# Feed-forward part with ScalarE and VectorE in written order, gelu and product written later, weight sums at a pair's first split

## The chip, the cores and the metric

The kernel runs on one core of one Trainium2 chip. Its time is the device time of one launch in microseconds, taken as the median of several runs. One more execution was recorded by the hardware profiler; all rows of the trace come from that one.

## The reference

Two layers of a decoder, 512 tokens, width 1024, all in float32. Each layer has a part with four token mixers and then a gated feed-forward part; only the second is touched here. `D_FF` is 2816, so gate and value have 22 blocks of 128 channels each.

```python
hf = rms_norm(x, norm_ffn_pre[l])
u = causal_depthwise_conv(hf @ ffn_w_up[l], ffn_conv_w[l], ffn_conv_b[l])   # 3 taps
gate, val = jnp.split(u, 2, axis=-1)
f = (jax.nn.gelu(gate, approximate=True) * val) @ ffn_w_down[l]
x = x + rms_norm(f, norm_ffn_post[l])
```

## The kernel before

**Split numbers.** Every float32 matmul is made of three: operands are split into a rounded high part (ScalarE, a copy) and the rest (VectorE, a subtraction), and hi x hi, lo x hi and hi x lo are summed in PSUM. Weights arrive by SP's DMA queue in units of 128x1024 in three `raw` buffers and are split into four pairs of buffers `whi`, `wlo`. `w_get` takes the next unit, `w_ahead(n)` writes the splits up to n units ahead, `w_split` does it. Activations are split by `hilo` (L316); `hT_hi` and `hT_lo` hold the normed input, channels on the partitions.

**Pairs.** The up projection runs over 22 pairs i = 0..21, one block of gate (s = 0) and one of value (s = 1). Pairs 0 and 1 are made by `head`, which works while the norm before is still coming in. Of the others, 8 are full pairs: two projections `proj` of 24 matmuls of 512 columns. The 12 pairs in `SEVEN` (i from 4 to 20, those not divisible by 3) are made by `seven`: the 2x2 block product (two halves of the channels, two halves of the tokens) by seven half products instead of eight (`product`, 12 matmuls of 256 columns). For that, sums of weight blocks are formed by POOL in `w_seven` (units `fs`, n = 0..3), and sums of input blocks in `forms(h)`, h = 0, 1, as tiles ta..tf, split into t1..t4 (forms d1, d2, d4, d3). Three banks take the products, named sa, sb, se; ScalarE copies an intermediate state of `ba` three times (L1392, L1399, L1405) before the next product is accumulated into it, and VectorE adds (L1396, L1410, L1416). The last two products of a seven-pair, `four` and `three`, are not made at once: they are put into `rest`, and `more()` takes one from it between the products of the next pair.

**After a pair**, `ffn_pair` (L1311) scales both banks on ScalarE (L1316), adds two taps each on VectorE (L1319, 4 in all), applies gelu on ScalarE (L1321) and multiplies on VectorE (L1322). `split_act` splits finished products already, up to six. The down projection is the function `boundary`, which also makes the norm and starts the next layer.

**Order.** SP's queue is always in the written order. For the other engines a planner (the Tile scheduler, with its own estimates of time) reorders what is written, unless a stretch is put under `manual_schedule`: then the engine's queue is in the written order. In the feed-forward part before, that holds for TensorE alone, from after pair 1 to the tail of the down projection; ScalarE, VectorE and POOL are in the planner's order. There are helpers for writing things later: `later(us, fn)` puts a piece into `due`, and `pump(us)`, called after some microseconds' worth of matmuls, counts it down and writes it when its time has come; `bg` is a queue of pieces that `pump` writes when a rough count of VectorE's work (`dve(us)`, `behind()`) is below a bound.

Of the kernel before, what the change touches and what calls it, by code (L numbers as in the profile page):

```python
# [21 lines left out]
NP_ = DFF // 128  # L22
# [54 lines left out]
SLACK0 = 0.6  # L77
SLACK2 = 1.5
MAXB = 1.5

SEVEN = {i for i in range(4, NP_ - 1) if i % 3}

# [23 lines left out]
def build(tc, x, wts, prm, gains, cst, out, order=None):  # L106
# [5 lines left out]
    with ExitStack() as ctx:  # L112
# [14 lines left out]
        def slot(w=512, dt=F32, name="g"):  # L127
            return pg.tile([128, w], dt, tag="g", bufs=NG, name=nm(name))
# [41 lines left out]
        def halves(i, *srcs):  # L170

            hi = pw.tile([128, WMAX], F32R, tag="whi", bufs=NSPL, name=nm("whi"))
            lo = pw.tile([128, WMAX], F32R, tag="wlo", bufs=NSPL, name=nm("wlo"))
            c = 0
            for s, n in srcs:
                A.activation(hi[:, c:c + n], s, AF.Copy)  # L176
                V.tensor_tensor(lo[:, c:c + n], s, f(hi[:, c:c + n]), op=ALU.subtract)  # L177
                c += n
            parts[i] = (hi, lo)

        def w_seven(i):


            _, p, n = order[i][1]
            if n == 0:
                sums[p] = [i]
                halves(i, (raw[i], 1024))
            elif n == 1:
                r1, r2 = raw.pop(sums[p].pop()), raw[i]
                s1, s2, s4 = slot(name="s1"), slot(name="s2"), slot(name="s4")  # L190
                sums[p] += [s4, i]
                G.tensor_tensor(s1, r2[:, 0:512], r2[:, 512:1024], op=ALU.add)  # L192
                G.tensor_tensor(s2, s1, r1[:, 0:512], op=ALU.subtract)
                G.tensor_tensor(r2[:, 0:512], r1[:, 0:512], r2[:, 0:512], op=ALU.subtract)  # L194
                G.tensor_tensor(s4, r1[:, 512:1024], s2, op=ALU.subtract)  # L195
                halves(i, (s2, 512), (s1, 512))
            elif n == 2:
                halves(i, (raw.pop(sums[p].pop()), 1024))
            else:
                halves(i, (sums.pop(p)[0], 512))  # L200

        def w_split(q, roomy=False):

# [112 lines left out]
        def hilo(src, scale=1.0, name="hl"):  # L316
            dve(0.62)
            hi = slot(dt=F32R, name=name + "h")
            lo = slot(dt=F32R, name=name + "l")
            if scale == 1.0:  # L320
                A.activation(hi, src, AF.Copy)
                V.tensor_tensor(lo, src, f(hi), op=ALU.subtract)
            else:
                A.activation(hi, src, AF.Copy, scale=scale)
                V.scalar_tensor_tensor(lo, src, scale, f(hi), op0=ALU.mult, op1=ALU.subtract)
            return hi, lo
# [269 lines left out]
        for l in range(L):  # L596
# [714 lines left out]
            def ffn_pair(i, bs):  # L1311
                w = lambda k, s: pr[:, P_FW + k * 44 + s * NP_ + i:P_FW + k * 44 + s * NP_ + i + 1]
                us = [slot(name="fu") for _ in range(2)]
                for s in range(2):
                    j = P_FB + s * NP_ + i
                    A.activation(us[s], bs[s], AF.Identity, scale=w(2, s), bias=pr[:, j:j + 1])  # L1316
                for d in (1, 2):
                    for s in range(2):
                        V.scalar_tensor_tensor(us[s][:, d:], bs[s][:, :512 - d], w(2 - d, s), us[s][:, d:],  # L1319
                                               op0=ALU.mult, op1=ALU.add)  # L1320
                A.activation(us[0], us[0], AF.Gelu_apprx_tanh)  # L1321
                V.tensor_tensor(us[1], us[0], us[1], op=ALU.mult)  # L1322
                fa[i] = us[1]

            hb = head(l, [("fu", 0), ("fu", NP_), ("fu", 1), ("fu", NP_ + 1)], hooks)
            ffn_pair(0, hb[0:2])
            ffn_pair(1, hb[2:4])
            ffn_order.enter_context(tc.manual_schedule(engines={E_T}))
            hb = None


# [1 line left out]
            def v2(t):  # L1333
                return t.rearrange("p (k t) -> p k t", k=2)
# [3 lines left out]
            def forms(h):  # L1338
                def block(t, k, q):
                    return f(t[:, k * 4 + h * 2:k * 4 + h * 2 + 2, q * 256:q * 256 + 256])  # L1340
                hi, lo = (lambda k, q: block(hT_hi, k, q)), (lambda k, q: block(hT_lo, k, q))
                a, b = slot(name="ta"), slot(name="tb")
                V.tensor_tensor(v2(a), hi(0, 1), hi(0, 0), op=ALU.subtract)
                V.tensor_tensor(v2(b), lo(0, 1), lo(0, 0), op=ALU.subtract)
                V.tensor_tensor(a, a, b, op=ALU.add)
                form["d1"].append(hilo(a, name="t1"))
                c = slot(name="tc")
                V.tensor_tensor(v2(c), hi(1, 1), v2(a), op=ALU.subtract)
                V.tensor_tensor(v2(c), v2(c), lo(1, 1), op=ALU.add)
                form["d2"].append(hilo(c, name="t2"))  # L1350
                d = slot(name="td")
                V.tensor_tensor(v2(d), hi(1, 0), v2(c), op=ALU.subtract)
                V.tensor_tensor(v2(d), v2(d), lo(1, 0), op=ALU.add)
                form["d4"].append(hilo(d, name="t4"))
                e, g = slot(name="te"), slot(name="tf")
                G.tensor_tensor(v2(e), hi(1, 1), hi(0, 1), op=ALU.subtract)
                G.tensor_tensor(v2(g), lo(1, 1), lo(0, 1), op=ALU.subtract)
                G.tensor_tensor(e, e, g, op=ALU.add)
                form["d3"].append(hilo(e, name="t3"))

            def side(n, kt):
                if n in form:
# [4 lines left out]
            def product(b, w, c, n, first):  # L1367

                o = b[:, 0:256]
                kw = {} if first else {"skip_group_check": True}  # L1370
                for kt in range(4):
                    hi, lo = side(n, kt)
                    k = c + kt * 128
                    mm(o, wc(w[0], k), hi, first and kt == 0, False, **kw)
                    mm(o, wc(w[0], k), lo, False, False, **kw)
                    mm(o, wc(w[1], k), hi, False, kt == 3, **kw)

            rest = []

# [4 lines left out]
            def seven(i):  # L1384


                ba, bb, be = bank("sa"), bank("sb"), bank("se")
                sa, sb = slot(name="ca"), slot(name="cb")
                L_, R_ = slice(0, 256), slice(256, 512)
                w0 = w_get(l, ("fs", i, 0))  # L1390
                product(ba, w0, 0, (0, 0), True)
                A.activation(sa[:, L_], ba[:, L_], AF.Copy)  # L1392
                more()
                w_ahead(2)
                product(bb, w0, 512, (1, 0), True)
                V.tensor_tensor(bb[:, L_], bb[:, L_], sa[:, L_], op=ALU.add)  # L1396
                w1 = w_get(l, ("fs", i, 1))
                product(ba, w1, 0, "d2", False)
                A.activation(sa[:, R_], ba[:, L_], AF.Copy)  # L1399
                w_ahead()  # L1400
                more()
                product(be, w1, 512, "d1", True)
                w2 = w_get(l, ("fs", i, 2))
                product(ba, w2, 0, "d3", False)
                A.activation(sb[:, L_], ba[:, L_], AF.Copy)  # L1405
                w_ahead()

                def four():
                    product(ba, w2, 512, "d4", False)
                    V.tensor_tensor(ba[:, R_], be[:, L_], sb[:, L_], op=ALU.add)  # L1410

                def three():
                    w3 = w_get(l, ("fs", i, 3))
                    product(be, w3, 0, (1, 1), False)
                    w_ahead(2)
                    V.tensor_tensor(bb[:, R_], be[:, L_], sa[:, R_], op=ALU.add)  # L1416
                    ffn_pair(i, [bb, ba])
                rest.extend((four, three))

            forms(0)  # L1420
            for i in range(2, NP_):
                if i == 3:
                    forms(1)
                if i in SEVEN:
                    seven(i)
                    continue
                bs = []
                for s in range(2):
                    b = bank()
                    run(proj(b, l, ("fu", s * NP_ + i)))  # L1430
                    bs.append(b)
                    more()
                ffn_pair(i, bs)
                if i >= 4:
                    split_act(fa, min(6, 2 * (i // 3)))
            while rest:
                more()
            form.clear()
            lastl = l == L - 1
            if not lastl:  # L1440
# [131 lines left out]
```

## Time and profile before

| | |
|---|---|
| time, median of 3 runs (lowest, highest) | 1957.84 us (1956.21, 1959.49) |
| the profiled execution: time, span | 1954.89 us, 1953.1 us |
| its granted TensorE clock, mean | 0.99 |
| busy: TensorE, VectorE, ScalarE, POOL | 97%, 73%, 49%, 16% |
| feed-forward part, layer 0: from the first projection of pair 2 to the down projection | 620.0 to 859.2 us |
| the same, layer 1 | 1587.0 to 1821.9 us |

A row of a group of instructions has line, engine, operation, output and input tiles, shape and count, then busy microseconds and mean nanoseconds of one, then the idle time of the engine just ahead of them and what ended it. A row of the timeline or of the chain begins with the start and the length in microseconds. A row of the waits gives the sum, the count and the longest. In the table of windows the columns are stretch, length, busy time (and count) of TensorE, its weight loads, VectorE, ScalarE and POOL, the granted clock, the DMA share and GB/s. Matmuls are pipelined: their listed length is longer than the distance from one to the next, so rates are taken from long stretches.

### The profile page before, as it was taken

The numbers are of one execution on the slowest core, as the hardware profiler recorded it, in microseconds if no ns is written. First come the engines' busy times: TensorE is split into PE (matmuls) and PEld (weight loads), VectorE is DVE, ScalarE is ACT, GpSimd is POOL, SyncE is SP. The second block draws the span as 40 slices with busy tenths as digits, with TensorE's granted clock in tenths as the row PEclk, the third lists the DMA queues.
The fourth block names the chain that finished last, engine by engine and source line by source line (L and its number), as shares of the span: only waits on it lengthen the run. The fifth ranks groups of instructions, "written<-read, shape, count | busy, mean of one in ns | idle before, by whom it ended". The sixth has DMA issues, their size and how long they took to land.

```text
span 1953.1 us, 27602 instructions
## 1 busy us (share of the span) xinstructions
PE 1885.1 (97%) x10236; PEld 1628.1 (83%) x10236; DVE 1418.7 (73%) x2546; ACT 965.1 (49%) x1840; POOL 312.2 (16%) x377
## 2 busy tenths in 40 slices
PE   7999999999999879999999999999999997999997
PEld 7988888888889778888898888888888897888886
DVE  6888789798558777764468887897975587667622
ACT  5557576623334455543345666775233435545521
POOL 1403300000004333400023033000000052243000
PEclk9999999999999999999999999999999998999999
DMA  8523311232353223234554233112323512223332
GB/s 291 154 76 98 108 57 55 68 98 87 102 192 106 65 87 98 87 112 140 160 188 141 72 103 108 49 58 73 97 81 118 206 66 87 87 87 99 128 119 76
DMA packets 74695, 209.10 MB, mean 107 GB/s; under 512 B 11072, under 2 KB 11456, under 8 KB 74560
## 3 DMA queue, kind: packets, MB, share of 16 engines
q1 hardware_dynamic: 67392, 192.65, 30.4%
q0 software_dynamic: 7168, 14.69, 3.0%
q8 instruction: 80, 1.31, 0.3%
q14 instruction: 55, 0.45, 0.1%
HBM read 184.23 MB, written 8.39 MB: 99 GB/s over the span
## 4 chain that ended last, share of the span: by engine, by line
PE 80%; issue 7%; DVE 6%; POOL 3%; ACT 3%; DMA 1%; SPq 0%; DVEq 0%; POOLq 0%; ACTq 0%
PE ps L293 43%; PE tk L293 15%; PE sa L293 5%; PE o L293 3%; PE hd L293 3%; PE se L293 2%; PE vt L293 2%; PE sB L293 1%; PE sA L293 1%; DVE fu L1319 1%; PE tr L382 1%; DVE wlo L233 1%; POOL raw L194 1%; POOL s L195 1%; ACT fu L1316 1%
## 5 line engine op out<-in xcount | busy, mean ns | idle before, releaser
L232 ACT ACTIVATE whi<-raw 128x1024 fp32r<-128x1024 f32 (+2 forms) x270 | 254.8, 948 | 483.7 <-PE ps L293 270.6
L233 DVE TENSOR_TENSOR wlo<-raw,whi 128x1024 fp32r<-128x1024 f32 (+2 forms) x270 | 297.9, 1107 | 243.0 <-ACT whi L232 241.2
L293 PE MATMUL ps<-hT_hi,whi 128*128 128x512 f32 x1104 | 438.5, 397 | 0.8 <-DVE ob L1092 0.8
L293 PE MATMUL ps<-hT_hi,wlo 128*128 128x512 f32 x1104 | 435.4, 394 | 0.0
L293 PE MATMUL ps<-hT_lo,whi 128*128 128x512 f32 x1104 | 434.0, 393 | 0.0
L293 PEld LDWEIGHTS ps<-hT_hi,wlo 128*128 128x128 f32 x1104 | 207.8, 188 | 47.1
L293 PEld LDWEIGHTS ps<-hT_hi,whi 128*128 128x128 f32 x1104 | 208.1, 188 | 43.9 <-DVE ob L1092 1.7
L293 PEld LDWEIGHTS ps<-hT_lo,whi 128*128 128x128 f32 x1104 | 208.0, 188 | 42.9
L895 DVE SCALAR_TENSOR_TENSOR acc<-ct,prm,acc 128x511 f32<-128x511 f32 (+14 forms) x240 | 175.6, 732 | 3.4
L293 PE MATMUL tk<-whi,fh 128*128 128x512 f32 x336 | 131.0, 390 | 0.0
L293 PE MATMUL tk<-whi,fl 128*128 128x512 f32 x336 | 130.8, 389 | 0.0
L293 PE MATMUL tk<-wlo,fh 128*128 128x512 f32 x336 | 130.8, 389 | 0.0
L177 DVE TENSOR_TENSOR wlo<-raw,whi 128x1024 fp32r<-128x1024 f32 x48 | 72.8, 1520 | 71.0 <-ACT whi L176 71.0
L348 POOL TENSOR_TENSOR sm<-sm,mhalf 128x1 f32<-128x1 f32 x32 | 22.2, 694 | 557.5 <-DVE sm L347 557.5
L176 ACT ACTIVATE whi<-raw 128x1024 fp32r<-128x1024 f32 x48 | 50.6, 1060 | 87.0 <-issue 30.3
L1052 ACT ACTIVATE P<-P,sm 128x256 f32<-128x256 f32 (+3 forms) x128 | 70.6, 554 | 29.7 <-DVE sm L1050 28.0
L929 POOL TENSOR_TENSOR sm<-sm,mhalf 128x1 f32<-128x1 f32 x8 | 6.1, 762 | 479.7 <-DVE sm L927 472.6
L192 POOL TENSOR_TENSOR s<-raw 128x512 f32<-128x512 f32 x24 | 32.7, 1361 | 265.6 <-DMA raw<-wts 265.6
L293 PEld LDWEIGHTS tk<-whi,fl 128*128 128x128 f32 x336 | 63.1, 188 | 13.2
L293 PEld LDWEIGHTS tk<-wlo,fh 128*128 128x128 f32 x336 | 63.1, 188 | 12.9
L293 PEld LDWEIGHTS tk<-whi,fh 128*128 128x128 f32 x336 | 63.1, 188 | 12.9
L293 PE MATMUL sa<-t2h,whi 128*128 128x256 f32 x96 | 32.2, 336 | 42.1 <-ACT ca L1392 42.1
(352 smaller groups left out, 4612.0 us busy)
## 6 DMA issues: line engine op xcount, KB each, us to landing
raw<-wts SPq DMA_DIRECT2D x260, 512.0 KB, 3.6
raw<-wts SPq DMA_DIRECT2D x66, 256.0 KB, 2.6
br<-wts SPq DMA_DIRECT2D x40, 256.0 KB, 6.2
xr<-x SPq DMA_DIRECT2D x16, 256.0 KB, 5.0
gain<-gains SPq DMA_DIRECT2D x16, 256.0 KB, 5.5
Q<-hlh POOLq DMA_DIRECT2D x64, 64.0 KB, 2.5
Q<-hll POOLq DMA_DIRECT2D x64, 64.0 KB, 2.9
raw<-wts SPq DMA_DIRECT2D x8, 408.0 KB, 5.1
```

What stands on the lines that cost most here:

```text
L176: A.activation(hi[:, c:c + n], s, AF.Copy)
L177: V.tensor_tensor(lo[:, c:c + n], s, f(hi[:, c:c + n]), op=ALU.subtract)
L192: G.tensor_tensor(s1, r2[:, 0:512], r2[:, 512:1024], op=ALU.add)
L194: G.tensor_tensor(r2[:, 0:512], r1[:, 0:512], r2[:, 0:512], op=ALU.subtract)
L195: G.tensor_tensor(s4, r1[:, 512:1024], s2, op=ALU.subtract)
L232: A.activation(hi[:, c:c + n], s, AF.Copy)
L233: V.tensor_tensor(lo[:, c:c + n], s, f(hi[:, c:c + n]), op=ALU.subtract)
L293: T.matmul(o, lhsT=lhsT, rhs=rhs, start=start, stop=stop, **kw)
L348: G.tensor_tensor(v[:, 1:2], v[:, 0:1], mhalf[:, 0:1], op=ALU.pow)
L382: T.transpose(bs[t, h][:, k * 128:k * 128 + 128], y[h][:, k * 128:k * 128 + 128], ident)
L895: V.scalar_tensor_tensor(acc[i][:, k:], ct[i][:, :512 - k], w[:, 30 - k:31 - k], acc[i][:, k:], op0=ALU.mult, op1=ALU.add)
L1052: A.activation(P[i], P[i], AF.Exp, bias=mn[:, i:i + 1], scale=-1.0, accum_out=sm[:, i:i + 1])
```

## The change

- ScalarE and VectorE are put in the written order too, and this begins ahead of pair 0's and pair 1's `ffn_pair`; it ends where TensorE's ended before, in the tail of the down projection.
- In `ffn_pair` the taps are written bank by bank, and gelu and product are written later: after 4.2 and 5.7 us worth of matmuls. `product` now calls `pump`, so that this count goes on.
- `w_seven` writes a seven-pair's four weight sums with its first split (n = 0) instead of its second, with the last two exchanged.
- `forms` puts its VectorE operations and splits into `bg`; both halves are written before pair 2, and what is left is written ahead of the first seven-pair.
- `four` and `three` of a seven-pair that is followed by a full pair are now made in the middle and at the end of that pair's first projection (before: after the first and after the second). `split_act` is written between the two projections. In `seven` one `w_ahead()` becomes `w_ahead(2)`, and in `three` L1416 is written ahead of `w_ahead(2)`.

```diff
--- before.py
+++ after.py
@@ -77,6 +77,9 @@
 SLACK0 = 0.6
 SLACK2 = 1.5
 MAXB = 1.5
+
+T_G = 4.2
+T_M = 5.7
 
 SEVEN = {i for i in range(4, NP_ - 1) if i % 3}
 
@@ -183,21 +186,21 @@
 
             _, p, n = order[i][1]
             if n == 0:
-                sums[p] = [i]
                 halves(i, (raw[i], 1024))
-            elif n == 1:
-                r1, r2 = raw.pop(sums[p].pop()), raw[i]
+                assert i + 1 in raw
+                r1, r2 = raw.pop(i), raw[i + 1]
                 s1, s2, s4 = slot(name="s1"), slot(name="s2"), slot(name="s4")
-                sums[p] += [s4, i]
                 G.tensor_tensor(s1, r2[:, 0:512], r2[:, 512:1024], op=ALU.add)
                 G.tensor_tensor(s2, s1, r1[:, 0:512], op=ALU.subtract)
+                G.tensor_tensor(s4, r1[:, 512:1024], s2, op=ALU.subtract)
                 G.tensor_tensor(r2[:, 0:512], r1[:, 0:512], r2[:, 0:512], op=ALU.subtract)
-                G.tensor_tensor(s4, r1[:, 512:1024], s2, op=ALU.subtract)
-                halves(i, (s2, 512), (s1, 512))
+                sums[p] = [i + 1, s4, s1, s2]
+            elif n == 1:
+                halves(i, (sums[p].pop(), 512), (sums[p].pop(), 512))
             elif n == 2:
-                halves(i, (raw.pop(sums[p].pop()), 1024))
+                halves(i, (raw.pop(sums[p][0]), 1024))
             else:
-                halves(i, (sums.pop(p)[0], 512))
+                halves(i, (sums.pop(p)[1], 512))
 
         def w_split(q, roomy=False):
 
@@ -1314,18 +1317,27 @@
                 for s in range(2):
                     j = P_FB + s * NP_ + i
                     A.activation(us[s], bs[s], AF.Identity, scale=w(2, s), bias=pr[:, j:j + 1])
-                for d in (1, 2):
-                    for s in range(2):
+                dve(3.0)
+                for s in range(2):
+                    for d in (1, 2):
                         V.scalar_tensor_tensor(us[s][:, d:], bs[s][:, :512 - d], w(2 - d, s), us[s][:, d:],
                                                op0=ALU.mult, op1=ALU.add)
-                A.activation(us[0], us[0], AF.Gelu_apprx_tanh)
-                V.tensor_tensor(us[1], us[0], us[1], op=ALU.mult)
-                fa[i] = us[1]
+
+                def gelu():
+                    A.activation(us[0], us[0], AF.Gelu_apprx_tanh)
+
+                def times():
+                    dve(0.7)
+                    V.tensor_tensor(us[1], us[0], us[1], op=ALU.mult)
+                    fa[i] = us[1]
+                later(T_G, gelu)
+                later(T_M, times)
 
             hb = head(l, [("fu", 0), ("fu", NP_), ("fu", 1), ("fu", NP_ + 1)], hooks)
+            ffn_order.enter_context(tc.manual_schedule(engines={E_T, E_A, E_V}))
+            clk["dve"] = clk["pe"]
             ffn_pair(0, hb[0:2])
             ffn_pair(1, hb[2:4])
-            ffn_order.enter_context(tc.manual_schedule(engines={E_T}))
             hb = None
 
 
@@ -1339,24 +1351,28 @@
                 def block(t, k, q):
                     return f(t[:, k * 4 + h * 2:k * 4 + h * 2 + 2, q * 256:q * 256 + 256])
                 hi, lo = (lambda k, q: block(hT_hi, k, q)), (lambda k, q: block(hT_lo, k, q))
-                a, b = slot(name="ta"), slot(name="tb")
-                V.tensor_tensor(v2(a), hi(0, 1), hi(0, 0), op=ALU.subtract)
-                V.tensor_tensor(v2(b), lo(0, 1), lo(0, 0), op=ALU.subtract)
-                V.tensor_tensor(a, a, b, op=ALU.add)
-                form["d1"].append(hilo(a, name="t1"))
-                c = slot(name="tc")
-                V.tensor_tensor(v2(c), hi(1, 1), v2(a), op=ALU.subtract)
-                V.tensor_tensor(v2(c), v2(c), lo(1, 1), op=ALU.add)
-                form["d2"].append(hilo(c, name="t2"))
-                d = slot(name="td")
-                V.tensor_tensor(v2(d), hi(1, 0), v2(c), op=ALU.subtract)
-                V.tensor_tensor(v2(d), v2(d), lo(1, 0), op=ALU.add)
-                form["d4"].append(hilo(d, name="t4"))
-                e, g = slot(name="te"), slot(name="tf")
-                G.tensor_tensor(v2(e), hi(1, 1), hi(0, 1), op=ALU.subtract)
-                G.tensor_tensor(v2(g), lo(1, 1), lo(0, 1), op=ALU.subtract)
-                G.tensor_tensor(e, e, g, op=ALU.add)
-                form["d3"].append(hilo(e, name="t3"))
+                a, b, c, d, e, g = (slot(name="t" + n) for n in "abcdef")
+                sub, add = ALU.subtract, ALU.add
+
+                def op(o, x, y, how):
+                    def go():
+                        dve(0.62)
+                        V.tensor_tensor(o, x, y, op=how)
+                    bg.append(go)
+                op(v2(a), hi(0, 1), hi(0, 0), sub)
+                op(v2(b), lo(0, 1), lo(0, 0), sub)
+                op(a, a, b, add)
+                op(v2(c), hi(1, 1), v2(a), sub)
+                op(v2(c), v2(c), lo(1, 1), add)
+                bg.append(lambda: form["d1"].append(hilo(a, name="t1")))
+                op(v2(d), hi(1, 0), v2(c), sub)
+                op(v2(d), v2(d), lo(1, 0), add)
+                bg.append(lambda: form["d2"].append(hilo(c, name="t2")))
+                G.tensor_tensor(v2(e), hi(1, 1), hi(0, 1), op=sub)
+                G.tensor_tensor(v2(g), lo(1, 1), lo(0, 1), op=sub)
+                G.tensor_tensor(e, e, g, op=add)
+                bg.append(lambda: form["d4"].append(hilo(d, name="t4")))
+                bg.append(lambda: form["d3"].append(hilo(e, name="t3")))
 
             def side(n, kt):
                 if n in form:
@@ -1374,6 +1390,7 @@
                     mm(o, wc(w[0], k), hi, first and kt == 0, False, **kw)
                     mm(o, wc(w[0], k), lo, False, False, **kw)
                     mm(o, wc(w[1], k), hi, False, kt == 3, **kw)
+                pump(1.42)
 
             rest = []
 
@@ -1397,7 +1414,7 @@
                 w1 = w_get(l, ("fs", i, 1))
                 product(ba, w1, 0, "d2", False)
                 A.activation(sa[:, R_], ba[:, L_], AF.Copy)
-                w_ahead()
+                w_ahead(2)
                 more()
                 product(be, w1, 512, "d1", True)
                 w2 = w_get(l, ("fs", i, 2))
@@ -1412,29 +1429,31 @@
                 def three():
                     w3 = w_get(l, ("fs", i, 3))
                     product(be, w3, 0, (1, 1), False)
+                    V.tensor_tensor(bb[:, R_], be[:, L_], sa[:, R_], op=ALU.add)
                     w_ahead(2)
-                    V.tensor_tensor(bb[:, R_], be[:, L_], sa[:, R_], op=ALU.add)
                     ffn_pair(i, [bb, ba])
                 rest.extend((four, three))
 
             forms(0)
+            forms(1)
             for i in range(2, NP_):
-                if i == 3:
-                    forms(1)
                 if i in SEVEN:
+                    while bg:
+                        bg.popleft()()
                     seven(i)
                     continue
                 bs = []
                 for s in range(2):
                     b = bank()
-                    run(proj(b, l, ("fu", s * NP_ + i)))
+                    for k, _ in enumerate(proj(b, l, ("fu", s * NP_ + i))):
+                        if k % 2 == 1 and s == 0:
+                            more()
                     bs.append(b)
-                    more()
+                    if s == 0 and i >= 4:
+                        split_act(fa, min(6, 2 * (i // 3)))
                 ffn_pair(i, bs)
-                if i >= 4:
-                    split_act(fa, min(6, 2 * (i // 3)))
-            while rest:
-                more()
+            flush()
+            assert not rest and not bg
             form.clear()
             lastl = l == L - 1
             if not lastl:
```

## The prediction

> **What bounds the kernel now.** I read the page first, for the engines:
>
> ```profile
> span 1953.1 us, 27602 instructions
> PE 1885.1 (97%) x10236; PEld 1628.1 (83%) x10236; DVE 1418.7 (73%) x2546; ACT 965.1 (49%) x1840; POOL 312.2 (16%) x377
> ```
>
> TensorE sets the time, so only its pauses and its slow stretches can be won. Then the waits, for the whole run and for each layer's feed-forward window (columns: total us, times, longest):
>
> ```profile
> PE sa L293 <- ACT ca L1392: 42.1, 12, 6.2
> ...
> PE sa L293 <- ACT ca L1392: 22.2, 6, 6.2
> ...
> PE sa L293 <- ACT ca L1392: 19.9, 6, 6.2
> ```
>
> All twelve pauses have one form: in the first of every two neighbouring seven-product pairs, product "d2" may not overwrite bank `ba` before ScalarE has copied its left half away (L1392). The chain shows one of them, and where the feed-forward part ends; the timeline shows where TensorE began it in each layer:
>
> ```profile
> 651.19 2.93 PE sa L293 x12
> 654.12 1.94 PE se L293 x12
> ...
> 784.84 4.32 issue
> 789.16 1.07 ACT whi L176
> 790.79 1.30 issue
> 793.89 1.45 ACT fu L1316 x2
> 795.66 1.70 PE sa L293 x12
> ...
> 798.80 4.30 PE sa L293 x36
> ...
> 810.26 5.60 PE ps L293 x24
> ...
> 859.20 111.56 PE tk L293 x492
> ```
>
> ```profile
> 620.03 0.40 PE L293 MATMUL ps<-hT_hi,whi 128*128 128x512 f32 x1
> 1587.04 0.40 PE L293 MATMUL ps<-hT_hi,whi 128*128 128x512 f32 x1
> 1821.92 1.16 PE tk L293 x5
> ```
>
> The unhindered rate is 4.30 us for 36 narrow and 5.60 for 24 wide matmuls. From pair 2 on a layer has 8 full pairs (16 x 5.60 = 89.6) and 12 seven-pairs (1008 narrow matmuls, 28 x 4.30 = 120.4): 210.0 us. It took 859.20 - 620.03 = 239.2 and 1821.92 - 1587.04 = 234.9. So 29.2 + 24.9 = 54.1 us are lost: 42.1 in pauses, 12.0 at a lower clock behind them. The windows show that clock:
>
> ```profile
> 651.00:656.00 5.00, 4.81 (x25) 4.81 (x26) 5.00 (x8) 4.00 (x8) 0.00 (x0) 0.59 0.12 15
> 793.00:800.00 7.00, 4.89 (x41) 4.68 (x40) 7.00 (x11) 5.18 (x10) 2.54 (x2) 1.00 0.48 150
> 827.00:834.00 7.00, 5.09 (x30) 4.95 (x29) 7.00 (x12) 4.33 (x9) 1.92 (x1) 0.76 0.38 140
> ```
>
> After the 6.2 us pause the clock was 0.59 and 24 narrow matmuls took 2.93 + 1.94 instead of 2.87: 2.0 us more. After a 2.1 us pause (793) it stayed at 1.00, after one of about 2 us (827) it fell to 0.76. The Trainium skill, "TensorE: Matmul & The Clock Gate", Part 1, gives an idle window of about 3.4 us before the clock halves; by that the short pause at 827 would have cost nothing further, and the row says that it did, so the row decides.
>
> **Why the copy is late.** In ScalarE's timeline, before L1392:
>
> ```profile
> 790.69 1.06 ACT L176 ACTIVATE whi<-raw 128x1024 fp32r<-128x1024 f32 x1 [0.47 <-PE se L293]
> 792.55 0.78 ACT L1316 ACTIVATE fu<-sb,prm 128x512 f32<-128x512 f32 x1 [0.80 <-DVE sb L1416]
> 793.23 0.77 ACT L1316 ACTIVATE fu<-sa,prm 128x512 f32<-128x512 f32 x1
> 793.89 1.45 ACT L1316 ACTIVATE fu<-ps,prm 128x512 f32<-128x512 f32 x2
> 795.21 0.39 ACT L1392 ACTIVATE ca<-sa 128x256 f32<-128x256 f32 x1
> ```
>
> ScalarE is 49% busy; it is not short of time. It stood behind weight splits that wait for a `whi` buffer still in use, then behind four scalings of two pairs at once: `three` of the old seven-pair and the full pair both end just before the new one starts.
>
> **The change, part by part.** Call one period F (full pair), C, D (seven-pairs), D' the D before. At the unhindered rate TensorE runs, from 0: F's first half 0 to 2.8, four(D') to 4.2, rest of that projection to 7.0, three(D') to 8.5, F's second projection to 14.1, then C's five products (last ends at 21.2), D(0,0) to 22.6, four(C), D(1,0), D d2 to 26.9, three(C) to 28.4, d1, d3 to 31.2. The written order of both queues follows from the new code. Prices, from the groups in 662 to 860 and (last row) the page's DMA issues:
>
> ```profile
> L177 DVE TENSOR_TENSOR wlo<-raw,whi 128x1024 fp32r<-128x1024 f32 x21 | 34.3, 1632 | 35.6 <-ACT whi L176 35.6
> L177 DVE TENSOR_TENSOR wlo<-s,whi 128x512 fp32r<-128x512 f32 x31 | 20.5, 677 | 0.0
> L233 DVE TENSOR_TENSOR wlo<-raw,whi 128x1024 fp32r<-128x1024 f32 x15 | 18.3, 1221 | 10.6 <-ACT whi L232 10.6
> L1319 DVE SCALAR_TENSOR_TENSOR fu<-sa,prm,fu 128x511 f32<-128x511 f32 (+1 forms) x22 | 16.2, 737 | 0.0
> L1322 DVE TENSOR_TENSOR fu<-fu,fu 128x512 f32<-128x512 f32 x16 | 13.8, 865 | 1.0 <-ACT fu L1321 0.5
> L1416 DVE TENSOR_TENSOR sb<-se,ca 128x256 f32<-128x256 f32 x12 | 5.1, 426 | 3.4 <-PE se L293 3.4
> L176 ACT ACTIVATE whi<-raw 128x1024 fp32r<-128x1024 f32 x20 | 21.2, 1061 | 42.7 <-issue 21.6 <-PE ps L293 13.8 <-PE sa L293 5.0
> raw<-wts SPq DMA_DIRECT2D x260, 512.0 KB, 3.6
> ```
>
> *Load.* A period gives VectorE 6 full splits (6 x 1.22), 6 half ones (6 x 0.68), 12 tap products (12 x 0.74), 3 gated products (at least 3 x 0.68, the uncontended length of a 512-wide operation) and 6 small sums (6 x 0.43): 24.9 of 31.2 us. Nothing is added, so order decides. 80% in strict order leaves about 6 us of slack.
>
> *L1392 of C.* Ahead of it on ScalarE now stand C1's and C2's splits, gelu(D') and F's two scalings. The splits' buffers are free by 8.5, so nothing there waits for F any more. VectorE reaches F's taps at about 14.8; F's second scaling follows the bank at 14.1 and ends at 14.9; L1392 follows product (0,0) at 15.5 and ends at 16.0. TensorE wants it at 16.9: about 1 us of slack, no pause. This takes away the steady pauses.
>
> *L1399 of C.* gelu(F) is now written ahead of it and waits for F's first two taps (16.1). L1399 follows d2 at 18.4, ends at 18.8, needed at 19.8: 1 us; F's taps could be 2.9 us later before it slips.
>
> *D0's split* is written behind L1399: ScalarE 18.8 to 19.8, VectorE to 21.1; D(0,0) needs the low part with its third matmul at 21.5. It is the tightest place: 0.4 us if VectorE is free and uncontended.
>
> *D2 and the next F split* (behind L1399 and three of D): done at 29.6 and 31.1, needed at 30.0 and 31.7: 0.4 and 0.6 us.
>
> *Banks.* L1410 must read `be` before three writes it. That distance shrinks in F from a whole second projection to half of one: ready at about 6, needed at 7.0.
>
> *Sums with the first split.* The four POOL operations come one split earlier; with the reordering `s4` is ready before the product that overwrites `raw`. SP's queue order stays; the first raw buffer is still read by the fourth operation, so D1's load starts at about 10, lands 3.6 later, and POOL works for D from 14 to 20. Its halves are wanted at 21.6. Cost nothing; if POOL slips by over a microsecond it shows as ScalarE waiting for L193.
>
> *Splits of gated products* (split_act): four in pair 6, two in pair 9, now inside the period, 4 x 0.68 on VectorE. They push D0 of seven-pair 7 past its need by about 1 us, once a layer.
>
> I take 0.5 us for each of the other five periods (between 0, where every slack holds, and 2.1, the pause that the row at 793 had at the same place), so 3.5 a layer.
>
> *The start.* Both `forms` now come before L1392 of pair 4. The chain before:
>
> ```profile
> 646.62 0.70 DVE td L1353
> ...
> 647.89 0.61 ACT t3h L321
> 648.50 1.04 ACT whi L176 x2
> 649.54 1.33 ACT fu L1316 x2
> 650.87 0.28 ACT ca L1392
> ```
>
> VectorE had been working without a break for it. In written order it must also have done, ahead of td(1), two half splits, one full split and pair 3's four taps: 1.2 + 1.2 + 2.7 = 5.1 (shown as later in the trace now); it is spared two waits of 0.7 for ScalarE, since `d` is written ahead of the t2 split. ScalarE in turn has its 2.4 us of splits and scalings behind it. So L1392 ends at 651.15 + 5.1 - 1.4 - 2.4 = 652.5, and the pause grows from 6.2 to about 7.6, plus 2.0 of clock: 9.6 a layer. Bounds: 6.2 (nothing gets later) and 11.3 (no relief).
>
> *The down projection* is in order too until its tail. Nothing there is late:
>
> ```profile
> 860.00:972.00 112.00, 112.00 (x500) 92.83 (x499) 52.83 (x70) 41.88 (x67) 2.09 (x3) 1.00 0.44 142
> ```
>
> VectorE at 47%, ScalarE at 37%, splits three units ahead: 0. If that cover were gone, a split late by x would cost x.
>
> **The sum.** Left per layer: 9.6 + 3.5 = 13.1. Won: 54.1 - 2 x 13.1 = 27.9. The profiled execution was 1954.89 (span 1953.1 and 1.8 around it), 0.15% under the median; 1957.8 - 27.9 = 1930 on the median's scale.
>
> **A rule that speaks against it.** VectorE operations beside POOL ones are longer here: the 1632 against the 1221 above, and 865 against 0.68. Over a layer that is 21 x 0.41 + 16 x 0.18 = 11.5 us, 1.9 a period. In the new order up to four such operations a period (two gated products, C0's and D0's low parts) fall into POOL's stretches, at 0.7 each 2.8, so 0.9 more, and at D0 it falls where there is no slack. The Trainium skill, "SBUF — State Buffer", Who interferes with whom, says that a VectorE instruction with two SBUF inputs and a GpSimd one that reads SBUF block each other fully; the 1632 agrees. If each period pays that 0.9 in full on top, 12 x 0.9 = 11 us go back: 1941.
>
> **The rivals.**
> 1. *Clean order* (0.15): no residue, first pause as before: 54.1 - 2 x 8.2 = 37.7 won, 1920; were the start to vanish as well, 1904. For it: VectorE has 6 us of slack a period. Against: three slacks of 0.4 to 0.6.
> 2. *Half the stalls stay* (0.20): port blocking at D0, or L1392 still late behind F's scalings. With 1.5 to 2.1 us in each period: 1941 to 1953. Here belongs also that the change does not cure what it aims at: F's scalings still stand ahead of L1392.
> 3. *Slower* (0.10): strict order makes gelu(F) hold L1399. VectorE would be late at F's taps; beyond 2.9 us each microsecond goes straight into TensorE's wait before d3. It decides from 27.9 / 12 = 2.3 us a period beyond that, so taps 5.2 late; at 3 us a period with 0.3 of clock it would be 1930 + 12 x 3.3 = 1970. For it: the four taps, two splits and a gated product come in one burst from 12 to 19. Against: 80% load.
>
> The forecast itself has 0.50 (own range 1918 to 1942), and 0.05 is no change: a run of rival 2 or 3 that ends within 0.2%, 3.9 us, about what a measurement of this kernel tells apart. Faster: 0.50 + 0.15 + 0.20 = 0.85. The range, 1908 to 1952, leaves out the best of rival 1 and the slow cases.
>
> **What would show it.** The wait "sa on L1392" falls from 42.1 to some 15 to 18 us, nearly all in two entries of 7 to 9 us; a small new wait of D(0,0) for L177; POOL's L192 early in each period; clock 1.00 in every stretch but the one behind pair 4. Wrong if ScalarE waits long for L1319 with L1399 behind it, if new entries of TensorE on L177 exceed 1 us a period, or if the first pause is beyond 11 us.

## The result, and the profile after

The changed kernel takes 1942.04 us (1939.32 to 1942.91) against 1957.03 in the same runs: ratio 0.992, interval 0.9903 to 0.9937. That is 15 us; 28 were forecast. From the page of the changed kernel:

```profile
PE 1880.2 (97%) x10236; PEld 1622.7 (84%) x10236; DVE 1437.0 (74%) x2546; ACT 955.6 (49%) x1840; POOL 313.6 (16%) x377
```

Its lines are renumbered: L1392, L1399, L1405, L1416, L1316, L1319, L1322 are now L1409, L1416, L1422, L1432, L1319, L1323, L1331. TensorE's waits, for each layer's feed-forward part:

```profile
PE sa L296 <- ACT ca L1409: 11.0, 1, 11.0
PE sa L296 <- ACT ca L1416: 3.5, 2, 3.2
PE sa L296 <- DVE wlo L180: 2.8, 4, 1.3
...
PE sa L296 <- ACT ca L1409: 9.5, 1, 9.5
PE sa L296 <- DVE wlo L180: 3.6, 5, 1.3
PE sa L296 <- ACT ca L1416: 3.5, 2, 3.2
```

Of the twelve pauses on the first copy, ten are gone. The two at pair 4 have grown from 6.2 to 11.0 and 9.5, and there are new ones on the second copy and on a low part. Where the parts begin (timeline) and end (chain):

```profile
620.82 0.40 PE L296 MATMUL ps<-hT_hi,whi 128*128 128x512 f32 x1
850.48 111.55 PE tk L296 x492
1577.38 0.40 PE L296 MATMUL ps<-hT_hi,whi 128*128 128x512 f32 x1
1808.46 91.60 PE tk L296 x404
```

The two layers take 229.7 and 231.1 us instead of 239.2 and 234.9, so 13.3 us less together, which is nearly the whole difference of the spans (13.5). Above twice the unhindered 210.0 there remain 40.7 us: 33.9 of pauses, and 6.8 that are put down to a lower clock. This sum of two lengths is used below for every kernel ("the part").

One steady period shows how strict order works. ScalarE's timeline:

```profile
781.98 0.78 ACT L1319 ACTIVATE fu<-sb,prm 128x512 f32<-128x512 f32 x1 [3.74 <-DVE sb L1432]
...
783.32 1.14 ACT L179 ACTIVATE whi<-s 128x512 fp32r<-128x512 f32 x2
```

and VectorE's:

```profile
781.51 0.43 DVE L1432 TENSOR_TENSOR sb<-se,ca 128x256 f32<-128x256 f32 x1
782.79 1.53 DVE L1323 SCALAR_TENSOR_TENSOR fu<-sb,prm,fu 128x511 f32<-128x511 f32 x2 [0.85 <-ACT fu L1319]
...
788.02 2.97 DVE L1323 SCALAR_TENSOR_TENSOR fu<-ps,prm,fu 128x511 f32<-128x511 f32 x4
...
792.70 1.98 DVE L180 TENSOR_TENSOR wlo<-raw,whi 128x1024 fp32r<-128x1024 f32 x1
```

ScalarE stands still for 3.74 us, up to 781.98, for three's sum. The next pair's two half splits stand behind it, though POOL has both of their inputs ready at 780.30 (L194, from 778.67 for 1.63 us). From 782.79 on VectorE has twelve microseconds of work without a gap, and D0's low part comes last (792.70 to 794.68): TensorE waits 0.48 us for it.

### The profile page after: what moved, and what is told of

It reads as the page before. It is cut to its first block, busy times and chain, and to the rows that moved or that the text cites. A ratio compares the mean times of both kernels' runs of the same rounds, so it can differ in the third digit from the quotient of the medians.

```text
span 1939.6 us, 27581 instructions
## 1 busy us (share of the span) xinstructions
PE 1880.2 (97%) x10236; PEld 1622.7 (84%) x10236; DVE 1437.0 (74%) x2546; ACT 955.6 (49%) x1840; POOL 313.6 (16%) x377
## 4 chain that ended last, share of the span: by engine, by line
PE 86%; DVE 9%; issue 2%; ACT 1%; DMA 1%; POOL 0%; SPq 0%; DVEq 0%; POOLq 0%; ACTq 0%
PE ps L296 45%; PE tk L296 16%; PE sa L296 5%; PE hd L296 5%; PE o L296 3%; PE se L296 3%; DVE wlo L180 3%; DVE fu L1323 2%; PE vt L296 2%; PE sB L296 1%; PE sA L296 1%; PE sb L296 1%; PE tr L385 1%; DVE fu L1331 1%; PE tB L1076 1%
## 5 line engine op out<-in xcount | busy, mean ns | idle before, releaser
L236 DVE TENSOR_TENSOR wlo<-raw,whi 128x1024 fp32r<-128x1024 f32 (+2 forms) x270 | 297.3, 1105 | 229.3 <-ACT whi L235 227.5
L1055 ACT ACTIVATE P<-P,sm 128x256 f32<-128x256 f32 (+3 forms) x128 | 70.6, 554 | 29.7 <-DVE sm L1053 28.0
L193 POOL TENSOR_TENSOR s<-raw 128x512 f32<-128x512 f32 x24 | 39.3, 1637 | 260.1 <-DMA raw<-wts 254.2
L580 POOL DMA_DIRECT2D Q<-hlh x64 | 31.6, 497 | 198.9 <-ACT hlh L324 189.8
L296 PE MATMUL hd<-hT_hi,bh 128*128 128x256 f32 x256 | 63.4, 285 | 0.0
```

The lines of the kernel that those rows point to most:

```text
L296: T.matmul(o, lhsT=lhsT, rhs=rhs, start=start, stop=stop, **kw)
L580: G.dma_start(f(dst[row:row + 32, :]), f(src[srow:srow + 32, :]))
L1055: A.activation(P[i], P[i], AF.Exp, bias=mn[:, i:i + 1], scale=-1.0, accum_out=sm[:, i:i + 1])
```

## The experiments

Ratios are to the kernel before, in the same runs. They answer four questions: order or move, POOL, the small slacks, the start.

**Order or move.** *order_only*, the kernel before plus

```diff
+            ffn_order.enter_context(tc.manual_schedule(engines={E_T, E_A, E_V}))
             ffn_pair(0, hb[0:2])
             ffn_pair(1, hb[2:4])
-            ffn_order.enter_context(tc.manual_schedule(engines={E_T}))
```

> The kernel before, with nothing changed but that ScalarE and VectorE are in the written order from pair 0 on. Theory O+M (order helps only with the pieces written where they fit): gelu stands right behind its own four taps and holds ScalarE for 3 us in each pair, L1392 gets later, pauses of 4 to 6 us in all twelve places, 1965 to 1990. Rival O alone (order is the whole gain): 1938 to 1946.

Measured 2014.09 us, ratio 1.0295 (1.0275 to 1.0314). On the old code, order alone costs 58 us: the waits on L1392 rise from 42.1 to 87.7. gelu stands right behind its taps, and the copy behind both (ScalarE's timeline, pair 7):

```profile
696.44 0.63 ACT L1321 ACTIVATE fu<-fu 128x512 f32<-128x512 f32 x1 [2.46 <-DVE fu L1319]
...
699.06 0.36 ACT L1392 ACTIVATE ca<-sa 128x256 f32<-128x256 f32 x1
```

*planner*, the changed kernel with

```diff
-            ffn_order.enter_context(tc.manual_schedule(engines={E_T, E_A, E_V}))
+            ffn_order.enter_context(tc.manual_schedule(engines={E_T}))
```

> The changed kernel, with ScalarE and VectorE given back to the planner in the feed-forward part; everything else of the change is kept (four and three moved, gelu and product later, sums first). Theory O (the strict order is what removes the steady pauses): the planner again puts scalings or splits ahead of the first copy, 4 to 6 pauses of 2 us a layer come back, 1948 to 1956 us. Rival M (the move of four and three is what counts, the order is not needed): 1934 to 1944, steady pauses on the copies below 8 us in sum.

Measured 1929.56 us, ratio 0.986 (0.9841 to 0.988): 12.5 us faster than with the order, and below the range of either theory. Its waits:

```profile
PE sa L296 <- ACT ca L1409: 13.6, 3, 11.3
...
PE sa L296 <- ACT ca L1409: 11.7, 2, 10.9
```

Hardly anything is left but the first pause. VectorE in the same period:

```profile
775.15 1.90 DVE L180 TENSOR_TENSOR wlo<-s,whi 128x512 fp32r<-128x512 f32 x2 [0.41 <-ACT whi L179]
776.98 0.42 DVE L1432 TENSOR_TENSOR sb<-se,ca 128x256 f32<-128x256 f32 x1
...
784.05 2.32 DVE L180 TENSOR_TENSOR wlo<-raw,whi 128x1024 fp32r<-128x1024 f32 x1
```

The pair's first product on TensorE, here and then in the changed kernel:

```profile
781.38 0.28 PE L296 MATMUL sa<-hT_hi,whi 128*128 128x256 f32 x1
```

```profile
786.82 0.28 PE L296 MATMUL sa<-hT_hi,whi 128*128 128x256 f32 x1
```

The next pair's two half splits stand ahead of three's sum here, and D0's low part is done at 786.37, 8.3 us earlier than with the order. Of this, 5.4 us are TensorE's own lead at this place (its pair begins at 781.38 and not 786.82); measured from the pair's beginning, the low part comes 2.9 us sooner, and TensorE does not wait for it. Theory O has fallen.

*move_only*, the kernel before plus

```diff
-                    run(proj(b, l, ("fu", s * NP_ + i)))
+                    for k, _ in enumerate(proj(b, l, ("fu", s * NP_ + i))):
+                        if k % 2 == 1 and s == 0:
+                            more()
                     bs.append(b)
-                    more()
```

> The kernel before with one edit: four and three are made in the middle and at the end of the full pair's first projection. Planner's order, gelu, product, sums and forms as before. Theory M (the move alone takes the steady pauses away; the rest of the change costs): first pause 6.2 a layer as before, the other ten pauses (29.7 us and some 8 of clock) nearly gone, 1918 to 1932. Rival (gelu and product later, or the sums first, are needed as well): 1940 to 1957.

Measured 1924.63 us, ratio 0.983 (0.9815 to 0.9844). This small edit gives 32 us, twice the whole change. Waits:

```profile
PE sa L293 <- ACT ca L1392: 10.2, 3, 6.3
...
PE sa L293 <- ACT ca L1392: 11.1, 3, 6.2
```

The pause at pair 4 is as before, the later ones are 3.9 and 4.9 us a layer, 8.8 of the 29.7 us before. So the move alone takes most of the steady pauses away; what else is in the change costs about 17 us in sum.

**POOL.** *sums_second*, the changed kernel with `w_seven` as it was before.

> The changed kernel with the weight sums written at the second split again. POOL's queue starts them when the raw units land, whichever split writes them, so theory: within 4 us of the changed kernel (1938 to 1946), POOL's first sum still waits for the DMA. Rival (the earlier writing is what makes the order possible): ScalarE waits for POOL at the halves, 1950 to 1960.

Measured 1942.49 us, ratio 0.9923 (0.9904 to 0.9942): no difference. The earlier sums buy nothing under strict order. Nor does the exchange of the last two: POOL is not in the written order, and in the changed kernel's trace L196 still runs ahead of L195.

*no_sums*, the changed kernel without POOL's four weight sums; three memsets take their place, so it does not compute the layer's result:

```diff
-                G.tensor_tensor(s1, r2[:, 0:512], r2[:, 512:1024], op=ALU.add)
...
+                for s_ in (s1, s2, s4):
+                    G.memset(s_, 0.01)
```

> The changed kernel with POOL's four sums of a seven-pair left out: three memsets take their place, so POOL writes and reads nothing, and the weights of the second to fourth unit are not the sums. Theory P (the remainder, 34 us of pauses, is in good part VectorE held up by POOL's reads): the 512-wide splits next to POOL fall from 1.7 to 0.7 us, first pause of a layer 11 to 6 or 7 us, steady ones 6 to 2 a layer, 1924 to 1933 us. Rival (strict order alone makes the pauses, POOL costs nothing): 1938 to 1943.

Measured 1923.37 us, ratio 0.9828 (0.9811 to 0.9845): 18.7 us less. VectorE's groups in layer 0's part, changed kernel and then this one:

```profile
L180 DVE TENSOR_TENSOR wlo<-raw,whi 128x1024 fp32r<-128x1024 f32 x24 | 36.2, 1508 | 17.8 <-ACT whi L179 17.8
L180 DVE TENSOR_TENSOR wlo<-s,whi 128x512 fp32r<-128x512 f32 x36 | 27.2, 794 | 1.0 <-ACT whi L179 1.0
L1331 DVE TENSOR_TENSOR fu<-fu,fu 128x512 f32<-128x512 f32 x22 | 24.0, 1097 | 0.0
```

```profile
L180 DVE TENSOR_TENSOR wlo<-raw,whi 128x1024 fp32r<-128x1024 f32 x24 | 29.3, 1221 | 20.8 <-ACT whi L179 20.8
L180 DVE TENSOR_TENSOR wlo<-s,whi 128x512 fp32r<-128x512 f32 x36 | 23.2, 685 | 3.8 <-ACT whi L179 3.6
L1329 DVE TENSOR_TENSOR fu<-fu,fu 128x512 f32<-128x512 f32 x22 | 14.9, 684 | 0.2 <-ACT fu L1325 0.2
```

Beside POOL's reads these three groups are 36.2 + 27.2 + 24.0 - 29.3 - 23.2 - 14.9 = 20.0 us longer in a layer. Without them the pauses behind pair 4 are 0.8 us a layer instead of 6.3 and 7.1, and the first is 9.1 and 9.0, not the 6 or 7 that were expected. The Trainium skill, "SBUF — State Buffer", Who interferes with whom, has a VectorE instruction with two SBUF inputs and a GpSimd one that reads SBUF exclude each other, while a GpSimd one that only writes does not; both sides of that are in these rows. Less than the lengthening is won at the first pause (1.9 and 0.5 us): in layer 0 the shorter operations of VectorE are followed by longer waits for ScalarE, 1.37 us ahead of a split at 627.76 and 1.57 ahead of taps at 633.21 and 644.19.

*planner_no_sums*, the same memsets with the planner's order (it leaves out the sums too).

> The planner's order with the change's writing, and POOL's four sums replaced by three memsets (the second to fourth weight units are then not the sums). Theory I (POOL's reads cost only where the order is strict, since the planner's order has other work to put there): 4 to 7 us from the first pauses alone, 1922 to 1926, so nearly the same as strict order without sums. Rival (POOL's blocking costs the same in any order): 18 us as under strict order, 1910 to 1914.

Measured 1922.16 us, ratio 0.9817 (0.9804 to 0.9831). Without POOL's reads the two orders are 1.2 us apart, which the intervals do not tell from nothing; with them 12.5. In *planner* VectorE's three groups are no shorter than in the strict order (1544, 862 and 1105 ns in layer 0), yet POOL's reads cost 7.4 us there and not 18.7. So theory I holds: the lengthening is at least as large, and what it costs depends on the order.

**The small slacks under strict order.** *gelu_later*: `T_G = 5.0`, `T_M = 7.0`.

> The changed kernel with gelu written after 5.0 instead of 4.2 and the product after 7.0 instead of 5.7 us of matmuls, so that in the seven-pair behind a full pair the copy L1416 stands ahead of gelu. Theory G (gelu holds that copy and, behind it, D0's split): L1416's 7 us of pauses vanish and most of the 6.4 us on the low part too, 1930 to 1936. Rival (VectorE's burst makes both late, gelu only stands there): 1939 to 1945.

Measured 1947.0 us, ratio 0.9948 (0.9932 to 0.9965), 5 us slower than the changed kernel. The pauses on the second copy vanish, but those on the low part grow from 6.4 to 15.0. In pair 7, D0's high part and low part, here and then in the changed kernel:

```profile
691.29 1.05 ACT L179 ACTIVATE whi<-raw 128x1024 fp32r<-128x1024 f32 x1
697.13 1.22 DVE L180 TENSOR_TENSOR wlo<-raw,whi 128x1024 fp32r<-128x1024 f32 x1
```

```profile
696.14 1.05 ACT L179 ACTIVATE whi<-raw 128x1024 fp32r<-128x1024 f32 x1
697.54 1.22 DVE L180 TENSOR_TENSOR wlo<-raw,whi 128x1024 fp32r<-128x1024 f32 x1
```

ScalarE is 4.9 us earlier and VectorE 0.41, which is no more than TensorE's own lead: the pair begins at 686.40 here and at 686.83 there. So VectorE's burst is the limit; gelu only stood in front of it. The rival holds, though its range ended at 1945.

*d0_early*: `w_ahead(3)` instead of `w_ahead(2)` behind L1409.

> The changed kernel with the second seven-pair's first split written one product earlier than its copy L1416 (ahead three instead of two after L1409). Theory: the pauses on the low part (6.4 us) vanish, those on L1416 stay or grow by up to 2 us, 1936 to 1941. Rival (VectorE is late by its load at that point, wherever the split is written): within 2 us of the changed kernel or slower.

Measured 1948.91 us, ratio 0.9954 (0.9939 to 0.9969), 7 us slower. The low part's pauses become 7.0 instead of 6.4, the second copy's 10.5 instead of 7.0. So writing D0's split earlier does not help either; that the burst is too long for its place, whatever stands last in it, fits both runs.

**The start.** *d2_first*: forms in the order of use,

```diff
+                while n in form and len(form[n]) < 2:
+                    bg.popleft()()
                 o = b[:, 0:256]
...
-                    while bg:
-                        bg.popleft()()
                     seven(i)
```

with d2's sums of both halves ahead of the others in `bg`.

> The changed kernel, strict order kept, with the sums of forms written in the order of their use: all for d2 of both halves first, the others just ahead of the product that reads them. Eight VectorE operations of 0.6 us leave the stretch ahead of the first copy. Theory (the first pause is VectorE's queue of forms): it falls from 11.0 and 9.5 to 4 to 6 us, 1930 to 1936. Rival (what is put off makes TensorE wait at d1, d3 or d4 of the same pair): 1938 to 1944.

Measured 1956.25 us, ratio 0.9995 (0.9985 to 1.0005): the whole gain is gone, which neither expectation had. The first pause falls to 4.6 and 3.3, but five more follow in the same pair. Layer 0:

```profile
PE sa L296 <- ACT t2h L324: 4.6, 1, 4.6
PE sa L296 <- ACT t4h L324: 4.5, 2, 3.5
PE sa L296 <- ACT ca L1425: 3.5, 2, 3.2
...
PE se L296 <- ACT t1h L324: 1.9, 1, 1.9
```

The pauses sum to 35.9 us over both layers, hardly more than the changed kernel's 33.9, but the part is 57.4 us above 420, not 40.7: beside the pauses 21.5 us are lost instead of 6.8. The window of 640 to 672 us, the stretch of these pauses, in this kernel and then in the changed one (the granted clock is the third column from the end, 0.76 and 0.84):

```profile
640.00:672.00 32.00, 19.54 (x103) 17.06 (x102) 20.74 (x32) 10.38 (x19) 0.00 (x0) 0.76 0.10 34
```

```profile
640.00:672.00 32.00, 20.96 (x150) 20.22 (x150) 23.68 (x36) 12.24 (x22) 0.33 (x1) 0.84 0.11 34
```

*planner_forms*: planner's order and `forms` as before, called ahead of pairs 2 and 3.

> The changed kernel without the strict order and with forms as before (no background queue, second half ahead of pair 3). Theory F (the first pause grows from 6 to 11 us by where the forms are written, not by the strict order): it is back at 6.2 to 6.6 a layer, the others stay at 1.6 a layer, 1918 to 1923 us. Rival (gelu, product and sums written elsewhere make it): first pause stays at 10 or more, 1927 to 1931.

Measured 1928.49 us, ratio 0.9851 (0.9838 to 0.9864). The first pause stays at 11.6 and 10.1, so theory F falls: it is not the place of the forms. What stands ahead of the second half's t2 in VectorE's timeline is this:

```profile
640.70 1.78 DVE L180 TENSOR_TENSOR wlo<-s,whi 128x512 fp32r<-128x512 f32 x1
...
646.77 1.21 DVE L180 TENSOR_TENSOR wlo<-raw,whi 128x1024 fp32r<-128x1024 f32 x1
651.08 0.69 DVE L325 TENSOR_TENSOR t2l<-tc,t2h 128x512 fp32r<-128x512 f32 x1 [0.69 <-ACT t2h L324]
```

In the kernel with the move alone t2 is done first, and the pause is 6.3:

```profile
645.70 0.69 DVE L322 TENSOR_TENSOR t2l<-tc,t2h 128x512 fp32r<-128x512 f32 x1 [0.70 <-ACT t2h L321]
```

In *planner_forms* four weight splits, 6.0 us, run between 635.57 and 647.98, ahead of the second half's t2; in *move_only* none runs from 630.99 up to it. In the changed kernel four run from 628.56 to 643.34, where the written order puts them; why the planner does it too (sums there earlier, or gelu and product later) was not separated.

*seven5*: the move alone, with `SEVEN` from 5, so that pair 4 is a full pair.

> The kernel before with only the move of four and three, and with pair 4 made as a full pair, so that the first seven-pair is 5 and VectorE has 11.2 us more for forms. Theory D (the first pause is VectorE's start-up work, about 8 us late against TensorE): the pause of 6.3 and its clock (2.0) vanish in both layers, at 1.2 us a layer for the eighth half product: 1908 to 1914. Rival (the pause is at the first seven-pair wherever that is, since its scalings stand ahead of the copy): 1925 to 1929.

Measured 1918.81 us, ratio 0.9799 (0.9785 to 0.9812). The first pause is 2.8 and 3.0 at pair 5 instead of 6.3 and 6.2 at pair 4. In the profiled executions the part falls from 445.0 to 435.7 us, the median time by only 5.8 us, which is between the two expectations. Theory D holds in part: eleven more microseconds shorten the pause, they do not end it.

*planner_forms_seven5*: both edits together.

> Planner's order, forms as before, the change's later gelu and product, its sums and its placing of four and three, and pair 4 as a full pair. By theories F and D together: 1904 to 1911, some 3 to 6 us better than the move with pair 4 full, since its later pauses are 1.6 instead of 4 us a layer. Rival: no better than that kernel within 2 us, or slower.

Measured 1911.92 us, ratio 0.976 (0.9747 to 0.9774), the fastest: 46 us less than before, 30 less than the changed kernel. Pauses of 4.1 and 3.3 us in the two layers are left, all on the first copy.

## Why the prediction was right or wrong

**The number: inside the range, and in part by luck.** The sum was 12 us too low: 1942.04 lies at the upper end of the forecast's own range (1942), where rival 2 begins and where the rule on POOL had put it (1941). It is luck that the sum is not further off, since the prediction never weighed what the move gives alone (32 us) against what the order costs (12.5). (By rival 2's own price of 2.1 us a period its upper end is 1930 - 7 + 12 x 2.1, about 1948, and not 1953.) Left over in both layers are 40.7 us, not 26.2: the first pauses are 5.3 us longer in sum than the terms said, the residue is 6.4 and the clock 2.8. Without POOL's reads 23.6 us are left, less than forecast. So what the sum lacks is the lengthening of VectorE's operations beside POOL, which it priced but kept out as a rule that speaks against it.

**What bounds it, and what can be won: right.** 54.1 us were lost, in pauses and clock; the best kernel here is 46 us faster.

**"This takes away the steady pauses" (L1392 of C): the effect was right, the cause was not.** The steady pauses on this copy went as forecast. But the step reckoned with the written order and the move together, and "order decides" gave the gain to the order. The paragraph ahead of it had named the true cause, that `three` and the full pair end just before the new pair starts, and rival 2 held that F's scalings would still stand ahead of the copy. The move of `four` and `three` alone brings 1924.63, and within the change the written order costs 12.5 us (1929.56 against 1942.04). I never asked what the planner would make of the new code.

**"Nothing is added, so order decides; about 6 us of slack": the slack was counted over a period, not at a place.** The 24.9 of 31.2 us is a load at lengths without POOL; in one period of the changed kernel (768 to 799 us) VectorE is busy for 26.2 of 31.0. And VectorE cannot spread it: after three's sum all comes in one burst. Rival 3 named that burst and gave it 0.10. The burst misses its place only at the lengths beside POOL: in *no_sums* the pauses behind pair 4 are 0.8 us a layer.

**Residue, 3.5 a layer forecast, 6.3 and 7.1 measured.** The term for D0 held: 2.8 and 3.6. At pair 7 the L1399 step with its 2.9 us of slack failed: gelu waited for its taps and the copy behind it came 3.2 us late. The four splits of gated products that the prediction named there took 2.49 us (from 685.70), as priced. Behind them stand weight splits beside POOL's sums. ScalarE's timeline, then VectorE's:

```profile
695.34 0.63 ACT L1327 ACTIVATE fu<-fu 128x512 f32<-128x512 f32 x1 [5.72 <-DVE fu L1323]
695.88 0.36 ACT L1416 ACTIVATE ca<-sa 128x256 f32<-128x256 f32 x1
```

```profile
688.10 3.48 DVE L180 TENSOR_TENSOR wlo<-s,whi 128x512 fp32r<-128x512 f32 x2
691.50 2.30 DVE L180 TENSOR_TENSOR wlo<-raw,whi 128x1024 fp32r<-128x1024 f32 x1
```

At 685 and 1221 ns, their means without POOL's reads, these would be 3.2 us shorter, as much as the pause; in *no_sums* the pause on the second copy is 0.2. That is rival 3's place, paid once a layer and not in every period, and its cause is the one that rival 2 names, port blocking by POOL.

**The start, 7.6 forecast, 11.0 and 9.5 measured.** The terms put the second half's td 5.1 - 1.4 = 3.7 us later; in layer 0 it ends at 655.33 and not 647.31, 7.2 us later when the part's own 0.8 is taken off. The relief of 2.4 us behind it held: the copy begins 1.2 us after td and not 3.6. So it is the 3.7 that was mis-sized. The chain, then VectorE's timeline:

```profile
654.63 0.70 DVE td L1360
...
656.51 0.28 ACT ca L1409
```

```profile
621.83 1.53 DVE L1323 SCALAR_TENSOR_TENSOR fu<-hd,prm,fu 128x511 f32<-128x511 f32 x2 [1.29 <-ACT fu L1319]
...
625.15 3.48 DVE L1331 TENSOR_TENSOR fu<-fu,fu 128x512 f32<-128x512 f32 x2
...
634.28 3.18 DVE L180 TENSOR_TENSOR wlo<-s,whi 128x512 fp32r<-128x512 f32 x2
```

Two half splits took 3.2 us, not 1.2, and two gated products 3.5, since they run beside POOL. And VectorE, which "had been working without a break" before, now waits twice 1.29 us for `head`'s banks (at 619.00 and 621.83), because the next split is written behind them. POOL is a little less than half of it: without its reads the first pauses are 9.1 and 9.0, so 2.9 of the 5.3 us remain. What these are made of was not separated.

**Sums with the first split: cost nothing, right** (1942.49 with them undone). That `s4` would be ready earlier by the exchange was wrong, since POOL is reordered.

**The rule that speaks against it: its price was right where it was put.** It gave 11 us for the periods; without POOL's reads the pauses behind pair 4 fall by 11.8 us in both layers. Outside of that price lie 2.4 us at the first pauses and 2.9 beside the pauses; the median falls by 18.7. The rule should have stood in the sum. What POOL's reads cost in the kernel before was not measured; on the new code the planner's order pays 7.4, so a cost seen in one order does not carry over to another.

**The down projection at 0: right.** It begins with 111.55 us of unbroken matmuls, 111.56 before.

**The signs.** The wait on the first copy fell to 20.5 us, not to 15 to 18. Of the signs of being wrong, the first pause beyond 11 us was barely met in layer 0 (11.04), and the wait of ScalarE with the second copy behind it came once a layer, at pair 7.

## What to carry to other kernels

Ask of a pause which piece of work ends too near to the one that waits, and move that piece, before an order is fixed: here two pieces moved by one edit gave 32 us, and the written order costs 12.5 in the changed kernel. If an engine at 80% load is to run in a written order, look for the longest stretch between its waits and count the burst behind it with the lengths that operations have beside their neighbours. A kernel with several edits is best tried edit by edit: here the others took back 17 of the 32 us that one of them gave.

## What the hardware showed that I had not expected

What a pause costs beside its own length differs widely. In *d2_first* 35.9 us of pauses came with 21.5 us more, in the changed kernel 33.9 with 6.8. Part of this is that the pauses of pair 4 are split: the window of 640 to 672 us stayed at 0.76, since the next pause came before the clock was back, or soon after. Part is not. The 3.2 us pause at pair 7 is the same in both kernels, and behind it the granted clock was 1.00 in the changed kernel's layer 0 (696 to 703 us) and 0.50 in *d2_first* (702 to 708); behind the same pause in the changed kernel's layer 1 it was 0.50 too (1653.8 to 1657.2). And *sums_second*, with 33.1 us of pauses split like those of the changed kernel, loses 9.9 beside them. What decides whether such a pause slows the clock was not found.

The Trainium skill, "TensorE: Matmul & The Clock Gate", Part 1, has the clock restored after about 3.4 us of steady work. In the changed kernel 17 slow matmuls stand behind the pause of 11.0 us, from 656.83 to 660.58, about 3.7 us, which agrees.
